# A four-layer decoder trunk on one core: the gate projection of the linear attention as seven products of halves

## The chip, the cores and the metric

The kernel runs on one core of one Trainium2 chip. The metric is the device time of one execution in microseconds (us). The engines are TensorE (PE; PEld is its weight load), VectorE (DVE), ScalarE (ACT), GpSimd (POOL) and SyncE (SP, which here only issues transfers).

## The reference, cut to what matters

Two decoder layers are computed for 256 positions of width 1024: first a gated linear attention (GLA) with a SwiGLU feed-forward network (FFN), then a block attention with its own FFN. The change touches only the gate `g` of the first layer:

```python
def gla_mixer(x, w_in, w_gk, b_gk, norm_g, w_out):
    q, k, v, g, gk_low = split_cols(x @ w_in, GLA_COLS)      # 512, 512, 1024, 1024, 16 columns
    ...
    o = from_heads(rms_norm(o.astype(x.dtype), norm_g)) * jax.nn.silu(g)
    return o @ w_out
```

So `g = x @ W` with x of 256 x 1024 and W of 1024 x 1024, all in float32.

## The kernel before

**Arithmetic.** A float32 product is made from three TensorE products of rounded numbers: each operand is split into a high part (a rounding copy on ACT) and a low part (a subtraction on DVE), and `mm3` sums high x high, low x high and high x low. One weight unit is 128 partitions x 1024 numbers (512 KB): one transfer by SP, one ACT copy (L265), one DVE subtraction (L266). The 256 positions are two row tiles t = 0, 1; columns come in blocks of 512.

**Order.** The kernel is written as a list of operations with reads and writes (`Plan.op`), and a planner (`Plan.emit`) orders each engine's queue ahead of time with costs written in the code: an operation takes the earliest start that its inputs, its engine and its buffers allow; ties go to what was written first; operations marked urgent may go ahead. Engines then run their queues in that fixed order. Buffers are 41 slots of 128 x 1024 numbers (`S`), eight PSUM banks (`acc` and `ps`, four each), and a buffer takes a slot only if enough are left for all unplaced buffers written before it. An accumulating transfer (`dma_add`) is issued by POOL; the planner gives it 1.3 us and lets its reader start 8 us later.

**The stage around the change**, in the order in which it is written: the values `v` block 0, the decay and keys and queries (up to L826), rotary tables, the second value block for row tile 0 (`v_block(1, 0)`), and then the loop at L881 over the row tiles: for t = 1 first `v_block(1, 1)`; the attention output `fo` into two `ps` banks (L891); its mean square (ACT L900, DVE L903, POOL L906); the two gate blocks `g_block` (24 matmuls each, then Silu on ACT, L878); the gated output `og` (DVE L916), its transposes (PE L925) and their split (ACT L929, DVE L933). The output projection `out_proj` with its eight weight rows `wo0` to `wo7` (split at L268, L269), a layer norm, and the FFN follow.

**The FFN already has the scheme that the change brings to the gates** (`seven`, L542): a product of a 2 x 2 block matrix by seven instead of eight block products (Winograd's form), with sums of x made by `x_sums` (DVE L458, L462, ACT L461) and sums of weights made in place, by DVE (`add_to`, L577) or by an accumulating transfer (`add_dma`, L583).

Of the kernel before, what the change touches and what calls it, by code (L numbers as in the profile page):

```python
# [12 lines left out]
ALU = mybir.AluOpType  # L13
# [3 lines left out]
P = 128  # L17
# [174 lines left out]
def kernel(ctx, tc, x, positions, gla_w_in, gla_w_gk, gla_b_gk, gla_norm_g, gla_w_out,  # L192
# [104 lines left out]
    def load_cols(name, w, c0):  # L297
        return [w_kcols(f"{name}{i}", w, 2 * i, 2, c0, 512) for i in range(KT // 2)]
# [11 lines left out]
    def transpose_split(src, dst, t, half, skey=None, dstf=None, dkey=None, n=4, keep=None):  # L310
        ps = pl.buf("ps", "tr")

        def tr():
            for j in range(n):
                k = 4 * half + j
                nc.tensor.transpose(ps.f[:, j * P:(j + 1) * P], src.f[:, k * P:(k + 1) * P], ident.f)  # L316
        pe(n * 256, tr, [(src, skey) if skey is not None else src, ident], [ps], urgent=True)

        def view(i):
            if dstf is not None:  # L320
                return dstf(i)
            return dst.ap[i][:, t, 4 * half:4 * half + 4, :]

        def hi():
            nc.scalar.copy(view(0), ps.f[:, 0:n * P].rearrange("p (k c) -> p k c", k=n))  # L325

        def lo():
            h, l = view(0), view(1)
            nc.vector.tensor_tensor(out=l, in0=ps.f[:, 0:n * P].rearrange("p (k c) -> p k c", k=n), in1=h.bitcast(F32),  # L329
                                    op=ALU.subtract)  # L330
        kh = dkey if dkey is not None else (t, half)
        if dstf is None:
            act(n * P, hi, [ps], [(dst, ("h",) + kh)], urgent=True)
            dve(n * P, lo, [ps, (dst, ("h",) + kh)], [(dst, ("l",) + kh)], urgent=True)
            if keep is not None:
                act(512, lambda: nc.scalar.copy(keep[t].f[:, 512 * half:512 * half + 512], ps.f), [ps],
                    [(keep[t], half)], urgent=True)
        else:
            dh, dl = dst
            act(n * P, hi, [ps], [(dh, kh)], urgent=True)  # L340
            dve(n * P, lo, [ps, (dh, kh)], [(dl, kh)], urgent=True)

    def Tk(T, t, k):
        return [(T, ("h", t, k // 4)), (T, ("l", t, k // 4))]
# [78 lines left out]
    def v_block(blk, t, T, ws, vt):  # L423
        ps = pl.buf("acc", f"v{blk}{t}")
        act_block(ps, T, ws, t)
        sl = slice(512 * blk, 512 * blk + 512)
        act(512, lambda: nc.scalar.copy(vt[t].f[:, sl], ps.f), [ps], [(vt[t], blk)])
# [249 lines left out]
    pl.op("SP", 0.8, lambda: None)  # L677
    load_x(0, 1, 2.9)
    for hf in range(2):
        transpose_split(xs[0], T0, 0, hf, skey=hf)  # L680
        if hf == 0:
            pl.op("PE", 0.6, busy(WARM[1]), [zeros, (xs[0], 0)], [junkps], urgent=True)
    for hf in range(2):
        load_x(1, hf, 2.9)
        transpose_split(xs[1], T0, 1, hf, skey=hf)
    wv0.append(split2("wv01", w0, 2, V0))
    wv0 += [w_kcols(f"wv0{i}", w0, 2 * i, 2, V0, 512) for i in range(2, KT // 2)]
    vps = [pl.buf("acc", f"v0{t}") for t in range(2)]
    for i in range(KT // 2):
        for t in range(2):  # L690
# [180 lines left out]
    og = [S_("og0"), S_("og1")]  # L871
    ogT = new_xT("ogT")

    def g_block(blk, t, ws):
        ps = pl.buf("acc", f"g{blk}{t}")
        act_block(ps, T0, ws, t)
        sl = slice(512 * blk, 512 * blk + 512)
        act(512, lambda: nc.scalar.activation(sg[t].f[:, sl], ps.f, AF.Silu), [ps], [(sg[t], blk)], table="silu")  # L878

    wgs = [load_cols("wg0", w0, G0), load_cols("wg1", w0, G0 + 512)]  # L880
    for t in range(2):  # L881
        if t == 1:
            v_block(1, 1, T0, wv1, v_sb)
        ob = [pl.buf("ps", f"o{t}{blk}") for blk in range(2)]
        for blk in range(2):
            def fo(blk=blk, t=t, ob=ob):
                for j in range(2):
                    h = 2 * blk + j
                    ops = [(scv(t), v_sb[t])] + ([(scv(2), v_sb[0])] if t else [])
                    for i, (s_, vt) in enumerate(ops):  # L890
                        nc.tensor.matmul(ob[blk].f[:, j * S:(j + 1) * S], s_[:, h, :], vt.f[:, h * S:(h + 1) * S],  # L891
                                         start=i == 0 and j == 0, stop=i == len(ops) - 1 and j == 1)
            pe(2048 * (1 + t), fo, [(scs[0], t), (v_sb[t], blk)] + ([(scs[1], 0), (v_sb[0], blk)] if t else []),
               [ob[blk]])
        ss, junk = pl.buf("m", "ss"), S_("junk")
        for blk in range(2):
            def fsq(blk=blk, ob=ob, ss=ss, junk=junk):
                for j in range(2):
                    h = 2 * blk + j
                    nc.scalar.activation(junk.f[:, h * S:(h + 1) * S], ob[blk].f[:, j * S:(j + 1) * S], AF.Square,  # L900
                                         accum_out=ss.f[:, h:h + 1])
            act(850, fsq, [ob[blk]], [(ss, blk), (junk, blk)])
        dve(10, lambda ss=ss: nc.vector.tensor_scalar(out=ss.f[:, 4:8], in0=ss.f[:, 0:4], scalar1=1.0 / GLA_DV,  # L903
                                                      scalar2=1e-6, op0=ALU.mult, op1=ALU.add),
            [(ss, 0), (ss, 1)], [(ss, 2)])
        pl.op("POOL", 0.6, lambda ss=ss: nc.gpsimd.tensor_tensor(  # L906
            out=ss.f[:, 8:12], in0=ss.f[:, 4:8], in1=mhalf.f.broadcast_to([P, 4]), op=ALU.pow),
            [(ss, 2), mhalf], [(ss, 3)])
        for blk in range(2):
            g_block(blk, t, wgs[blk])  # L910
        for blk in range(2):
            for j in range(2):
                def fog(blk=blk, j=j, t=t, ob=ob, ss=ss):
                    h = 2 * blk + j
                    hs = slice(h * S, (h + 1) * S)
                    nc.vector.scalar_tensor_tensor(out=og[t].f[:, hs], in0=ob[blk].f[:, j * S:(j + 1) * S],  # L916
                                                   scalar=ss.f[:, 8 + h:9 + h], in1=sg[t].f[:, hs],
                                                   op0=ALU.mult, op1=ALU.mult)
                dve(256, fog, [ob[blk], (ss, 3), (sg[t], blk)], [(og[t], (blk, j))], urgent=True)
            ps = pl.buf("ps", "trg")  # L920

            def trg(ps=ps, src=og[t], blk=blk):
                for j in range(4):
                    k = 4 * blk + j
                    nc.tensor.transpose(ps.f[:, j * P:(j + 1) * P], src.f[:, k * P:(k + 1) * P], ident.f)  # L925
            pe(4 * 256, trg, [(og[t], (blk, 0)), (og[t], (blk, 1)), ident], [ps], urgent=True)

            def gh(ps=ps, t=t, blk=blk):
                nc.scalar.copy(ogT.ap[0][:, t, 4 * blk:4 * blk + 4, :], ps.f.rearrange("p (k c) -> p k c", k=4))  # L929

            def gl(ps=ps, t=t, blk=blk):
                ks = slice(4 * blk, 4 * blk + 4)
                nc.vector.tensor_tensor(out=ogT.ap[1][:, t, ks, :], in0=ps.f.rearrange("p (k c) -> p k c", k=4),  # L933
                                        in1=ogT.ap[0][:, t, ks, :].bitcast(F32), op=ALU.subtract)
            act(512, gh, [ps], [(ogT, ("h", t, blk))], urgent=True)
            dve(512, gl, [ps, (ogT, ("h", t, blk))], [(ogT, ("l", t, blk))], urgent=True)

    gb = load_ln(0, 0)
    T1 = new_xT("xT1")
# [163 lines left out]
```

## Time and profile before

| | |
|---|---|
| median of 3 runs | 581.41 us (581.38 to 582.15) |
| the profiled execution | 580.57 us, of which the span from first to last instruction is 578.8 us |
| PE busy | 568.6 us, 98% of the span |
| DVE busy | 518.8 us, 90% |
| ACT busy | 352.5 us, 61% |
| granted TensorE clock | 0.998 of full speed |

PE and DVE are the two engines to watch. Busy shares are means over the span; the gate stage, which the change rewrites, is about 33 us of it.

### The profile page before, as it was taken

The page shows a single profiled execution, that of the slowest core. Times are in us where ns is not written, and L with a number is a line of the kernel's source. Part 1 is how long each engine was busy: PE and PEld are TensorE (multiplying, and loading weights), DVE is VectorE, ACT ScalarE, POOL GpSimd, SP SyncE. Part 2 cuts the span into 40 slices and gives each one's busy share as a digit, 9 for nine tenths or more (in the row PEclk, how much of TensorE's full clock was granted, in tenths as well). Part 3 has the DMA queues.
Part 4 walks back from the last instruction along what each step waited for, and adds up shares of the span by engine and source line. Part 5 has one row for each costly group of instructions (what it writes and reads, how often), then busy time and mean ns, then how long its engine had stood idle before and what let it go on. Part 6 is the DMA issues. An engine that isn't in the chain of part 4 may idle for free.

```text
span 578.8 us, 8048 instructions
## 1 busy us (share of the span) xinstructions
PE 568.6 (98%) x2980; PEld 485.6 (84%) x2980; DVE 518.8 (90%) x644; ACT 352.5 (61%) x469; POOL 45.3 (8%) x41
## 2 busy tenths in 40 slices
PE   9999999999999999999999999999999999999994
PEld 8898888888878888889889999888888788888883
DVE  5799467798999999999998789988989999999986
ACT  5696555346758586867454365734495767575720
POOL 1016000010010101000000000000101000010001
PEclk9999999999999999999999999999999999999999
DMA  9994286347896978869667445626867887877601
GB/s 289 352 327 145 76 265 244 110 129 234 265 217 224 257 236 239 209 215 285 215 212 228 160 144 179 208 74 218 215 203 221 213 286 176 307 179 236 183 1 72
DMA packets 57465, 119.38 MB, mean 206 GB/s; under 512 B 5265, under 2 KB 10801, under 8 KB 57426
## 3 DMA queue, kind: packets, MB, share of 16 engines
q1 hardware_dynamic: 51586, 108.84, 56.6%
q0 software_dynamic: 5408, 9.44, 10.1%
q10 hardware_dynamic: 432, 0.59, 0.3%
q8 instruction: 23, 0.38, 0.3%
q14 instruction: 16, 0.13, 0.1%
HBM read 117.81 MB, written 1.05 MB: 205 GB/s over the span
## 4 chain that ended last, share of the span: by engine, by line
PE 76%; DVE 9%; DMA 7%; ACT 3%; issue 3%; POOL 1%; DVEq 0%; ACTq 0%; SPq 0%
PE fy L303 6%; PE fy L301 6%; PE fy L302 6%; PE pa L560 4%; PE pa L559 4%; PE pa L557 4%; PE y L303 3%; PE y L302 3%; PE y L301 3%; DMA d0r<-in_ffn_w_down 2%; PE tr L316 2%; PE pc L557 2%; PE pc L560 2%; PE pc L559 2%; DVE A L577 2%
## 5 line engine op out<-in xcount | busy, mean ns | idle before, releaser
L577 DVE TENSOR_TENSOR A<-A,X 128x1024 f32<-128x1024 f32 x54 | 64.4, 1217 | 0.0
L583 POOL DMA_DIRECT2D X<-in_ffn_w_gu x18 | 22.2, 1261 | 261.2 <-PE fy L302 90.5
L325 ACT CAST xT<-tr 128x512 fp32r<-128x512 f32 x16 | 9.1, 590 | 31.1 <-PE tr L316 31.0
L372 POOL TENSOR_TENSOR st<-st,mhalf 128x1 f32<-128x1 f32 x8 | 7.6, 956 | 200.1 <-DVE st L370 200.1
L509 ACT CAST C0h<-X 128x1024 fp32r<-128x1024 f32 x10 | 10.5, 1051 | 16.8 <-DMA X<-in_ffn_w_gu 12.3
L509 ACT CAST B0h<-A 128x1024 fp32r<-128x1024 f32 x10 | 10.5, 1053 | 10.7 <-DVE A L577 10.7
L509 ACT CAST G0h<-A 128x1024 fp32r<-128x1024 f32 x10 | 10.5, 1052 | 6.8 <-DVE A L577 6.8
L509 ACT CAST A0h<-A 128x1024 fp32r<-128x1024 f32 x10 | 10.5, 1052 | 5.7 <-DMA A<-in_ffn_w_gu 5.5
L620 ACT ACTIVATE e<-pa 128x512 f32<-128x512 f32 (+1 forms) x10 | 5.5, 555 | 11.5 <-PE pa L560 11.5
L316 PEld LDWEIGHTS tr<-ident,e 128*128 128x128 f32 x72 | 8.7, 140 | 4.4 <-DVE e L621 1.9
L316 PE MATMUL tr<-ident,e 128*128 128x128 f32 x72 | 11.3, 274 | 1.0 <-DVE e L621 1.0
L509 ACT CAST D0h<-A 128x1024 fp32r<-128x1024 f32 x10 | 10.5, 1052 | 2.8 <-DVE A L577 2.8
L510 DVE TENSOR_TENSOR D0l<-A,D0h 128x1024 fp32r<-128x1024 f32 x10 | 12.2, 1219 | 0.0
L510 DVE TENSOR_TENSOR G0l<-A,G0h 128x1024 fp32r<-128x1024 f32 x10 | 12.2, 1218 | 0.0
L510 DVE TENSOR_TENSOR A0l<-A,A0h 128x1024 fp32r<-128x1024 f32 x10 | 12.2, 1218 | 0.0
L510 DVE TENSOR_TENSOR E0l<-X,E0h 128x1024 fp32r<-128x1024 f32 x10 | 12.2, 1218 | 0.0
L510 DVE TENSOR_TENSOR F0l<-X,F0h 128x1024 fp32r<-128x1024 f32 x10 | 12.2, 1218 | 0.0
L510 DVE TENSOR_TENSOR C0l<-X,C0h 128x1024 fp32r<-128x1024 f32 x10 | 12.2, 1217 | 0.0
L510 DVE TENSOR_TENSOR B0l<-A,B0h 128x1024 fp32r<-128x1024 f32 x10 | 12.2, 1216 | 0.0
L329 DVE TENSOR_TENSOR xT<-tr,xT 128x512 fp32r<-128x512 f32 x16 | 10.7, 684 | 1.5 <-ACT xT L325 0.9
L916 DVE SCALAR_TENSOR_TENSOR og<-o,ss,sg 128x256 f32<-128x256 f32 x8 | 3.6, 478 | 9.2 <-ACT sg L878 9.2
L364 DVE BATCH_NORM_STATS2 st<-r 128x6 f32<-128x512 f32 x16 | 11.1, 693 | 0.5
(1012 smaller groups left out, 2249.7 us busy)
## 6 DMA issues: line engine op xcount, KB each, us to landing
X<-in_ffn_w_gu SPq DMA_DIRECT2D x54, 512.0 KB, 4.8
A<-in_ffn_w_gu SPq DMA_DIRECT2D x18, 512.0 KB, 4.3
X<-in_ffn_w_gu POOLq DMA_DIRECT2D x18, 512.0 KB, 7.6
lng<-in_ln_g SPq DMA_DIRECT2D x4, 512.0 KB, 3.8
lnb<-in_ln_b SPq DMA_DIRECT2D x4, 512.0 KB, 5.4
x<-in_x SPq DMA_DIRECT2D x4, 256.0 KB, 3.8
fg00r<-in_ffn_w_gu SPq DMA_DIRECT2D x2, 512.0 KB, 6.6
fg01r<-in_ffn_w_gu SPq DMA_DIRECT2D x2, 512.0 KB, 7.0
```

Of the source, the lines that this page charges most:

```text
L301: nc.tensor.matmul(ps, lh, rh, start=start, stop=False)
L302: nc.tensor.matmul(ps, ll, rh, start=False, stop=False)
L303: nc.tensor.matmul(ps, lh, rl, start=False, stop=stop)
L316: nc.tensor.transpose(ps.f[:, j * P:(j + 1) * P], src.f[:, k * P:(k + 1) * P], ident.f)
L364: nc.vector.bn_stats(st.f[:, 6 * hf:6 * hf + 6], r.f[:, sl])
L509: act(1024, lambda: nc.scalar.copy(hi.r, raw.f), [raw], [hi])
L510: dve(1024, lambda: nc.vector.tensor_tensor(out=lo.r, in0=raw.f, in1=hi.f, op=ALU.subtract), [raw, hi], [lo])
L557: nc.tensor.matmul(ps.f[:, lo_], sh, wh.r[:, cs], start=first and q == 0 and j == 0, stop=False, skip_group_check=True)
L559: nc.tensor.matmul(ps.f[:, lo_], sl_, wh.r[:, cs], start=False, stop=False, skip_group_check=True)
L560: nc.tensor.matmul(ps.f[:, lo_], sh, wl.r[:, cs], start=False, stop=last_ and (q, j) == (units - 1, nk - 1), skip_group_check=True)
L577: dve(1024, lambda q=q, other=other: nc.vector.tensor_tensor(out=raws[q].f, in0=raws[q].f, in1=other.f, op=ALU.add), [raws[q], other], [ra ...
L583: nc.gpsimd.dma_start(uv(raws[q], n), unit(kh, gu, q, c0, n), accum_op=ALU.add)
```

## The change

The gate product is cut into halves: x into row tiles (t) and halves of its 1024 columns, W into halves of its rows (kh) and column blocks (cb). Instead of `g_block` for each t and cb (four blocks of 24 matmuls), `gate_seven` makes seven products of 12 matmuls, named after their left side (`a00`, `a01`, `s1`, `s2`, `s4`, `s3`, `a11`; `s` are sums of x). Three PSUM banks (pa, pb, pc) hold them. The sums of x are made by the FFN's `x_sums` from float32 copies of the transposed x, which ACT takes at the start (`xi32`). W's four quarters are used as seven right sides: three plain, four sums. Three of the four sums are accumulating transfers from memory (two units each, by POOL), one is a pair of DVE additions. Each right side is split anew into high and low parts. The second value block for t = 1, the gated output for t = 0 and the attention output for t = 1 come after the fifth product (`between`), and the first `fo` stays ahead of the gates.

```diff
+    xi32, x_t = [S_("x32i"), S_("x32j")], {}
...
-        transpose_split(xs[0], T0, 0, hf, skey=hf)
+        x_t[0, hf] = transpose_split(xs[0], T0, 0, hf, skey=hf)
...
+    for (t, hf), ps in x_t.items():
+        act(512, lambda t=t, hf=hf, ps=ps: nc.scalar.copy(xi32[t].f[:, 512 * hf:512 * hf + 512], ps.f),
+            [ps, wv0[3][0]], [(xi32[t], hf)])
...
-    def g_block(blk, t, ws):
-        ps = pl.buf("acc", f"g{blk}{t}")
-        act_block(ps, T0, ws, t)
-        sl = slice(512 * blk, 512 * blk + 512)
-        act(512, lambda: nc.scalar.activation(sg[t].f[:, sl], ps.f, AF.Silu), [ps], [(sg[t], blk)], table="silu")
-
-    wgs = [load_cols("wg0", w0, G0), load_cols("wg1", w0, G0 + 512)]
-    for t in range(2):
-        if t == 1:
-            v_block(1, 1, T0, wv1, v_sb)
+    def gate_seven(xsum, between):
+        pa, pc, pb = pl.buf("acc", "ga"), pl.buf("acc", "gc"), pl.buf("acc", "gb")
+        e1, e2 = sg
...
+        def load(kh, cb):
+            raws = [S_(f"gr{kh}{cb}{q}") for q in range(2)]
+            for q in range(2):
+                dma(lambda q=q: nc.sync.dma_start(uv(raws[q]), unit(kh, cb, q)), 512, [], [raws[q]])
+            return raws
+
+        def parts(raws):
+            out_ = []
+            for raw in raws:
+                hi, lo = S_("gwh", True), S_("gwl", True)
+                act(1024, lambda raw=raw, hi=hi: nc.scalar.copy(hi.r, raw.f), [raw], [hi])
+                dve(1024, lambda raw=raw, hi=hi, lo=lo: nc.vector.tensor_tensor(
+                    out=lo.r, in0=raw.f, in1=hi.f, op=ALU.subtract), [raw, hi], [lo])
+                out_.append((hi, lo))
+            return out_
+
+        def add(raws, others):
+            for r_, o_ in zip(raws, others):
+                dve(1024, lambda r_=r_, o_=o_: nc.vector.tensor_tensor(out=r_.f, in0=r_.f, in1=o_.f, op=ALU.add),
+                    [r_, o_], [r_])
+
+        def add_dma(raws, kh, cb):
+            for q in range(2):
+                dma_add(lambda q=q: nc.gpsimd.dma_start(uv(raws[q]), unit(kh, cb, q), accum_op=ALU.add), [raws[q]],
+                        [raws[q]])
+
+        def product(ps, left, ws, first, last_):
+            st, rd = lhs(left)
+            for q, (wh, wl) in enumerate(ws):
...
+                pe(6 * 512, f, rd + [wh, wl], [ps])
...
+        w00 = load(0, 0)
+        product(pa, "a00", parts(w00), True, False)
+        keep_(pa, e1, 0)
+        add_dma(w00, 0, 1)
+        w10 = load(1, 0)
+        product(pb, "a01", parts(w10), True, True)
+        combine(e1, 0, pb, ALU.add)
+        silu(e1, 0)
+        w11 = load(1, 1)
+        product(pc, "s1", parts(w00), True, False)
+        keep_(pc, e2, 0)
+        add(w00, w11)
+        w11s = parts(w11)
+        add_dma(w11, 0, 1)
+        product(pa, "s2", parts(w00), False, False)
+        keep_(pa, e1, 1)
+        add_dma(w00, 1, 0)
+        product(pc, "s4", w11s, False, True)
+        combine(e1, 1, pc, ALU.subtract)
+        silu(e1, 1)
+        between()
+        product(pa, "s3", parts(w11), False, False)
+        combine(e2, 0, pa, ALU.subtract, flip=True)
+        silu(e2, 0)
+        product(pa, "a11", parts(w00), False, True)
+        silu(e2, 1, pa)
...
+    heads = {0: head_out(0)}
+    xsum = x_sums(xi32)
+
+    def between():
+        v_block(1, 1, T0, wv1, v_sb)
+        gated(0, *heads[0])
+        heads[1] = head_out(1)
+    gate_seven(xsum, between)
+    gated(1, *heads[1])
```

`head_out` and `gated` hold the code of the old loop's first and second half. `keep_` is an ACT copy of a PSUM bank (128 x 512), `combine` a DVE operation with one PSUM and one SBUF input (128 x 512), `silu` an ACT activation; all three are urgent.

## Rows read from the trace of the kernel before

**Rows 1.** The page: busy time, share and instructions of each engine.
```profile
PE 568.6 (98%) x2980; PEld 485.6 (84%) x2980; DVE 518.8 (90%) x644; ACT 352.5 (61%) x469; POOL 45.3 (8%) x41
```
**Rows 2.** The longest waits of PE after its start: total, times, longest.
```profile
PE tr L316 <- DVE e L621: 1.0, 2, 0.6
PE scx L824 <- POOL kx L797: 0.4, 1, 0.4
```
**Rows 3.** Busy time of each engine in stretches between stages.
```profile
20.00:43.00 23.00, 23.00 (x184) 22.36 (x184) 20.38 (x33) 19.57 (x22) 2.19 (x5) 1.00 0.98 328
43.00:57.50 14.50, 14.06 (x96) 12.89 (x95) 14.50 (x18) 9.74 (x12) 9.09 (x2) 1.00 0.42 145
57.50:90.30 32.80, 32.80 (x150) 27.28 (x150) 17.15 (x21) 18.10 (x34) 2.04 (x2) 1.00 0.60 197
90.30:119.00 28.70, 28.70 (x133) 23.43 (x132) 22.95 (x34) 12.07 (x16) 1.98 (x2) 1.00 0.50 166
119.00:150.00 31.00, 31.00 (x146) 25.74 (x145) 29.01 (x34) 20.24 (x28) 2.58 (x2) 1.00 0.64 185
150.00:260.00 110.00, 109.41 (x496) 90.09 (x495) 109.81 (x109) 77.29 (x89) 8.58 (x7) 1.00 0.80 231
```
**Rows 4.** Timeline of PE in the gate stage (start, duration, line, operation).
```profile
64.13 0.39 PE L301 MATMUL g<-wg10h,xT 128*128 128x512 f32 x1
...
69.57 0.60 PE L925 MATMUL trg<-ident,og 128*128 128x128 f32 x4
...
75.98 0.59 PE L891 MATMUL o<-v,sc 128*128 128x256 f32 x2
...
79.24 0.58 PE L301 MATMUL g<-wg00h,xT 128*128 128x512 f32 x1
...
90.33 0.60 PE L925 MATMUL trg<-ident,og 128*128 128x128 f32 x4
```
**Rows 5.** Timeline of DVE: successive operations of each size, and the first FFN split.
```profile
58.49 1.21 DVE L266 TENSOR_TENSOR wg13l<-wg13r,wg13h 128x1024 fp32r<-128x1024 f32 x1
59.62 1.27 DVE L269 SCALAR_TENSOR_TENSOR wo0l<-wo0r,normg,wo0h 128x1024 fp32r<-128x1024 f32 x1
...
126.43 0.68 DVE L462 TENSOR_TENSOR s3hl<-s,s3hl 128x512 fp32r<-128x512 f32 x1
127.03 0.68 DVE L534 TENSOR_TENSOR sil<-pu,sil 128x512 f32<-128x512 f32 x1
```
**Rows 6.** Timeline of ACT: the decay weights, successive splits, a PSUM copy.
```profile
13.32 1.06 ACT L707 CAST wgkhl<-wgkr 128x1024 fp32r<-128x1024 f32 x1 [0.17 <-DMA wgkr<-in_gla_w_in]
...
47.86 1.04 ACT L265 CAST wg10h<-wg10r 128x1024 fp32r<-128x1024 f32 x1
48.80 1.04 ACT L265 CAST wg11h<-wg11r 128x1024 fp32r<-128x1024 f32 x1
...
108.41 0.59 ACT L336 COPY x32a<-tr 128x512 f32<-128x512 f32 x1
```
**Rows 7.** Timeline of PE: first reader of the decay weights.
```profile
19.23 2.08 PE L718 MATMUL gk<-xT,wgkhl 128*128 128x256 f32 x16
```
**Rows 8.** Line 583, the FFN's accumulating transfers: POOL's issue, and from issue to landing.
```profile
L583 POOL DMA_DIRECT2D X<-in_ffn_w_gu x18: 1203/1207/1392, 126.0 to 538.9; - x18
...
DMA to landing us min/median/max: 5.9/7.6/10.9
```
**Rows 9.** Timeline of POOL before the gate stage.
```profile
42.56 5.60 POOL L794 COPY kx<-ke 128x256 f32<-128x256 f32 x1
49.15 3.94 POOL L797 COPY kx<-qd 128x256 f32<-128x256 f32 x1 [0.99 <-DVE qd L775]
```
**Rows 10.** Timeline of SP's issues: the last weight row of the output projection.
```profile
74.85 0.38 SPq L262 DMA_DIRECT2D wo7r<-in_gla_w_out  x1
```
**Rows 11.** Timeline of DVE in the FFN: the split D1.
```profile
142.37 1.22 DVE L510 TENSOR_TENSOR D1l<-A,D1h 128x1024 fp32r<-128x1024 f32 x1
```
**Rows 12.** Timeline of PE in the FFN: its use of D1's low part.
```profile
148.09 0.39 PE L560 MATMUL pa<-D1l,s2hl 128*128 128x512 f32 x1
```

More of the change, by code (lines that the diff above doesn't have):

```diff
@@ L341, in transpose_split @@
             dve(n * P, lo, [ps, (dh, kh)], [(dl, kh)], urgent=True)
+        return ps
     def Tk(T, t, k):
@@ L684 @@
         load_x(1, hf, 2.9)
-        transpose_split(xs[1], T0, 1, hf, skey=hf)
+        x_t[1, hf] = transpose_split(xs[1], T0, 1, hf, skey=hf)
     wv0.append(split2("wv01", w0, 2, V0))
     wv0 += [w_kcols(f"wv0{i}", w0, 2 * i, 2, V0, 512) for i in range(2, KT // 2)]
+    for (t, hf), ps in x_t.items():
+        act(512, lambda t=t, hf=hf, ps=ps: nc.scalar.copy(xi32[t].f[:, 512 * hf:512 * hf + 512], ps.f),
+            [ps, wv0[3][0]], [(xi32[t], hf)])
     vps = [pl.buf("acc", f"v0{t}") for t in range(2)]
@@ L872, with lhs, unit, uv @@
     ogT = new_xT("ogT")
-    def g_block(blk, t, ws):
-        ps = pl.buf("acc", f"g{blk}{t}")
-        act_block(ps, T0, ws, t)
-        sl = slice(512 * blk, 512 * blk + 512)
-        act(512, lambda: nc.scalar.activation(sg[t].f[:, sl], ps.f, AF.Silu), [ps], [(sg[t], blk)], table="silu")
-    wgs = [load_cols("wg0", w0, G0), load_cols("wg1", w0, G0 + 512)]
-    for t in range(2):
-        if t == 1:
-            v_block(1, 1, T0, wv1, v_sb)
+    def gate_seven(xsum, between):
+        pa, pc, pb = pl.buf("acc", "ga"), pl.buf("acc", "gc"), pl.buf("acc", "gb")
+        e1, e2 = sg
+        def lhs(n):
+            if n[0] == "s":
+                return (lambda k: (xsum[n].r[:, k * P:(k + 1) * P], xsum[n].r[:, 512 + k * P:512 + (k + 1) * P]),
+                        [(xsum[n], 0), (xsum[n], 1)])
+            t, kh = int(n[1]), int(n[2])
+            return (lambda k: (T0.ap[0][:, t, 4 * kh + k, :], T0.ap[1][:, t, 4 * kh + k, :]),
+                    [(T0, ("h", t, kh)), (T0, ("l", t, kh))])
+        def unit(kh, cb, q):
+            k0 = 4 * kh + 2 * q
+            return w0[k0 * P:(k0 + 2) * P, G0 + 512 * cb:G0 + 512 * cb + 512].rearrange("(k p) c -> p k c", p=P)
+        def uv(b):
+            return b.f.rearrange("p (k c) -> p k c", k=2)
+        def load(kh, cb):
[23 more added lines that the diff above has]
+            for q, (wh, wl) in enumerate(ws):
+                def f(q=q, wh=wh, wl=wl):
+                    for j in range(2):
+                        sh, sl_ = st(2 * q + j)
+                        cs = slice(512 * j, 512 * j + 512)
+                        nc.tensor.matmul(ps.f, sh, wh.r[:, cs], start=first and q == 0 and j == 0, stop=False,
+                                         skip_group_check=True)
+                        nc.tensor.matmul(ps.f, sl_, wh.r[:, cs], start=False, stop=False, skip_group_check=True)
+                        nc.tensor.matmul(ps.f, sh, wl.r[:, cs], start=False, stop=last_ and q == 1 and j == 1,
+                                         skip_group_check=True)
+                pe(6 * 512, f, rd + [wh, wl], [ps])
+        def keep_(ps, dst, j):
+            sl = slice(512 * j, 512 * j + 512)
+            act(512, lambda: nc.scalar.copy(dst.f[:, sl], ps.f), [ps], [(dst, j)], urgent=True)
+        def combine(dst, j, ps, op, flip=False):
+            sl = slice(512 * j, 512 * j + 512)
+            def f():
+                a0, a1 = (dst.f[:, sl], ps.f) if flip else (ps.f, dst.f[:, sl])
+                nc.vector.tensor_tensor(out=dst.f[:, sl], in0=a0, in1=a1, op=op)
+            dve(512, f, [ps, (dst, j)], [(dst, j)], urgent=True)
+        def silu(dst, j, ps=None):
+            sl = slice(512 * j, 512 * j + 512)
+            act(512, lambda: nc.scalar.activation(dst.f[:, sl], ps.f if ps else dst.f[:, sl], AF.Silu),
+                [ps] if ps else [(dst, j)], [(dst, j)], table="silu", urgent=True)
+        w00 = load(0, 0)
[24 more added lines that the diff above has]
+        silu(e2, 1, pa)
@@ L884, with head_out, fo @@
+    def head_out(t):
         ob = [pl.buf("ps", f"o{t}{blk}") for blk in range(2)]
         for blk in range(2):
-            def fo(blk=blk, t=t, ob=ob):
+            def fo(blk=blk):
                 for j in range(2):
@@ L896, with fsq @@
         for blk in range(2):
-            def fsq(blk=blk, ob=ob, ss=ss, junk=junk):
+            def fsq(blk=blk):
                 for j in range(2):
@@ L902 @@
             act(850, fsq, [ob[blk]], [(ss, blk), (junk, blk)])
-        dve(10, lambda ss=ss: nc.vector.tensor_scalar(out=ss.f[:, 4:8], in0=ss.f[:, 0:4], scalar1=1.0 / GLA_DV,
-                                                      scalar2=1e-6, op0=ALU.mult, op1=ALU.add),
+        dve(10, lambda: nc.vector.tensor_scalar(out=ss.f[:, 4:8], in0=ss.f[:, 0:4], scalar1=1.0 / GLA_DV,
+                                                scalar2=1e-6, op0=ALU.mult, op1=ALU.add),
             [(ss, 0), (ss, 1)], [(ss, 2)])
-        pl.op("POOL", 0.6, lambda ss=ss: nc.gpsimd.tensor_tensor(
+        pl.op("POOL", 0.6, lambda: nc.gpsimd.tensor_tensor(
@@ L907, with gated, fog @@
             out=ss.f[:, 8:12], in0=ss.f[:, 4:8], in1=mhalf.f.broadcast_to([P, 4]), op=ALU.pow),
             [(ss, 2), mhalf], [(ss, 3)])
+        return ob, ss
+    def gated(t, ob, ss):
         for blk in range(2):
-            g_block(blk, t, wgs[blk])
-        for blk in range(2):
+            part = blk ^ t
             for j in range(2):
-                def fog(blk=blk, j=j, t=t, ob=ob, ss=ss):
+                def fog(blk=blk, j=j, part=part):
                     h = 2 * blk + j
                     hs = slice(h * S, (h + 1) * S)
+                    gs = slice(512 * part + j * S, 512 * part + (j + 1) * S)
@@ L916, in fog @@
                     nc.vector.scalar_tensor_tensor(out=og[t].f[:, hs], in0=ob[blk].f[:, j * S:(j + 1) * S],
-                                                   scalar=ss.f[:, 8 + h:9 + h], in1=sg[t].f[:, hs],
+                                                   scalar=ss.f[:, 8 + h:9 + h], in1=sg[t].f[:, gs],
                                                    op0=ALU.mult, op1=ALU.mult)
-                dve(256, fog, [ob[blk], (ss, 3), (sg[t], blk)], [(og[t], (blk, j))], urgent=True)
+                dve(256, fog, [ob[blk], (ss, 3), (sg[t], part)], [(og[t], (blk, j))], urgent=True)
@@ L920, with trg, gh @@
             ps = pl.buf("ps", "trg")
-            def trg(ps=ps, src=og[t], blk=blk):
+            def trg(ps=ps, blk=blk):
                 for j in range(4):
                     k = 4 * blk + j
-                    nc.tensor.transpose(ps.f[:, j * P:(j + 1) * P], src.f[:, k * P:(k + 1) * P], ident.f)
+                    nc.tensor.transpose(ps.f[:, j * P:(j + 1) * P], og[t].f[:, k * P:(k + 1) * P], ident.f)
             pe(4 * 256, trg, [(og[t], (blk, 0)), (og[t], (blk, 1)), ident], [ps], urgent=True)
-            def gh(ps=ps, t=t, blk=blk):
+            def gh(ps=ps, blk=blk):
@@ L929, in gh, with gl @@
                 nc.scalar.copy(ogT.ap[0][:, t, 4 * blk:4 * blk + 4, :], ps.f.rearrange("p (k c) -> p k c", k=4))
-            def gl(ps=ps, t=t, blk=blk):
+            def gl(ps=ps, blk=blk):
                 ks = slice(4 * blk, 4 * blk + 4)
```

## The prediction, as recorded before the run

> **What bounds the kernel now.** I read the page's busy times first. PE is busy 568.6 of 578.8 us [rows 1]: whatever shortens the kernel must take work from PE or one of its few pauses. The waits of PE come next: apart from its start it stood still 1.0 us for two DVE results in the FFN and 0.4 us for a POOL copy just ahead of the gate stage [rows 2]. Then the busy times by stage. In the gate stage (57.5 to 90.3 us) PE is busy all 32.80 us, DVE only 17.15 and ACT 18.10; up to 119 us, through the output projection and the layer norms, PE is still full and DVE has 22.95 of 28.7. Two neighbours look different: from 43 to 57.5 DVE is full (14.50 of 14.50), and in the FFN from 150 to 260 both are, PE 109.41 and DVE 109.81 of 110 [rows 3]. So matmuls taken out of the gates count in full, if DVE, which pays for them, gets its extra work done in the idle time between 57.5 and 119 us and enters the FFN no later than PE does.
>
> **What is removed.** The gates now take 2 row tiles x 2 column blocks x 8 row blocks x 3 = 96 matmuls of 128x512; seven products of 4 x 3 make 84. Twenty-four of them took 64.13 to 69.57 us [rows 4], 0.2267 us each: 12 x 0.2267 = 2.72 us less on PE. Transposes, `fo` and the value block only change place.
>
> **What is added on DVE.** Splits go from 8 to 14 units, +6; the weight addition is 2 operations of the same size. Successive ones start 1.13 us apart [rows 5]: 8 x 1.13 = 9.0 us. `x_sums` has 8 operations of half the size and `combine` 3; those start 0.60 us apart [rows 5]: 11 x 0.60 = 6.6. Together 15.7 us. (A `combine` has one operand in PSUM, as the row at 127.03 has.) The idle time between 57.5 and 119 us is 15.65 + 5.75 = 21.4 us [rows 3]; the stretch shrinks by 2.72, so about 3.0 us of slack stay. It fits, barely. The cover is this idle time alone: what doesn't find its place there arrives late in the FFN. There DVE idled another 1.99 us before 150 [rows 3], and its split D1, ended at 143.6, is read at 148.09 [rows 11, 12], a lead of 4.5 us that can be eaten before PE stops.
>
> **What is added on ACT.** Six splits at 0.94 us and eleven half-size copies (4 `xi32`, 4 in `x_sums`, 3 `keep_`) at 0.59 [rows 6]: 5.6 + 6.5 = 12.1 us. ACT idles 4.76 us from 43 to 57.5 and 14.7 us in the gate stage [rows 3]; hidden. The `xi32` copies come early: 4 x 0.59 = 2.4 us ahead of the decay weights' copy, which then starts at 15.7 instead of 13.32 and ends at 16.8 [rows 6]; PE first reads these at 19.23 [rows 7]. It costs nothing within that margin of 2.4 us.
>
> **Where x_sums goes.** Its inputs are there from about 16 us on, so the planner lets it run wherever DVE is free. From 20 to 43 us DVE idles 2.6 us [rows 3], half of what it needs (4.8); the rest falls into the full stretch 43 to 57.5. What is queued behind it there: keys, the copies kx on POOL (5.60 and 3.94 us, the second ending at 53.1 [rows 9]) and PE's `scx`, which already waits 0.4 us [rows 2]. On the other side DVE has six splits to make before 59.6 instead of eight, 2.3 us less. Bounds: from the 0.4 us gained to 2.2 us (4.8 - 2.6) lost; I take 0, since the planner can place the second half of `v_block(1, 0)` in front.
>
> **Accumulating transfers.** Three sums in two units each are 6 issues on POOL of 1.21 us, 7.3 us; POOL is busy 2.04 us in the stage [rows 3, 8]. Each lands 5.9 to 10.9 us after its issue, median 7.6 [rows 8]. They make a chain, and PE needs something else to do meanwhile. In times of the kernel before: POOL is free of kx at 53.1 [rows 9]; w00's two accumulations land at 60.7 and 61.9; two splits, some 3.2 us with ACT's part: s1 ready at about 65. Addition of w11, 2.3 us: 67.3. Splits: s2 ready at about 69.6. Then w00's second accumulation, to 78.4, and a11 ready at about 81. For w11 the accumulation starts at 67.3 and lands at 76.1: s3 ready at about 78. PE: a00 and a01 (24 matmuls, 5.4 us) and a half of `fo` end at about 63.6; `v_block(1, 1)` has all inputs and fills 5.4 us to 69.0; s1, s2, s4 at 2.72 each end at 77.2. So s1 has 4 us of slack, s2 some 2 us, s3 comes about 1 us late, and a11, which the transposes (0.9) and the second `fo` (3.26 us, 75.98 to 79.24 in [rows 4]) can precede, has some 3 us. The second `fo` is no filler any earlier: the four `ps` banks are two for the first `fo`, held until its gates are through, and two reserved for the transposes. Stall in the stage: from 0 to 1 us by these rows, and by the longest landing (10.9) more, which is a rival. I take 0.4, what the wait for kx costs today.
>
> **The end of the stage.** The last gates are off the path: row tile 0 of the output projection needs only `gated(0)`. The weight rows `wo` get their slots later than now (the last is issued at 74.85 [rows 10]), because unplaced gate parts reserve slots ahead of them; wv1's eight slots come free at about 69 in compensation, and DVE needs 1.13 to 1.21 us a row where PE uses 1.4 (six matmuls). I take 0 and count what goes wrong there under the first rival. Memory traffic rises by four units (12 instead of 8); the queues have room here (197 GB/s against 328 from 20 to 43 us [rows 3]).
>
> **Sum.** -2.72 + 0.4 = -2.3 us. The profiled execution took 580.57, so it would take 578.3; the median of the runs is 0.84 above it, so the median goes to 579.1. About 0.2% (1.2 us) is what can be told from no change.
>
> **The rivals.**
>
> *DVE becomes the bound.* DVE's idle time between dependent steps doesn't vanish because there is work elsewhere: while it waits for accumulations it can only take what has a slot, and the `wo` rows have none yet. If half of the gate stage's 15.65 us stays idle, 7.8 instead of 3.0, DVE enters the FFN 4.8 us late; 2.0 are absorbed there, 2.8 fall on the lead of 4.5 us. PE stalls 0 to 2.8 us: 579.1 to 581.9. Against it: the lead is larger than the rest.
>
> *The accumulations starve (slower).* POOL may be slow while DVE runs without pause: its plain copies of 128x256 took 5.60 and 3.94 us while DVE was full [rows 3, 9]. If each accumulation takes the longest 10.9 us instead of 7.6, the two in series on w11 bring s3 to about 84.6 against PE's 77.2; `v_block(1, 1)` is used up and the queue is fixed, so PE waits up to 7.4 us less what the planner's own 9.3 us had put ahead of s3 (some 3.4 us): 4 us. 581.41 - 2.72 + 4 + 0.4 = 583.1; it decides from 1.5 us a transfer on. Against it: issues of 1.20 to 1.39 us and a median of 7.6 us in an FFN whose DVE is 99.8% busy [rows 3, 8]. The Trainium skill has a rule for this (SBUF — State Buffer, section SBUF: two separate sides): a transfer issued by GpSimd may sit idle because its descriptors can't be written while VectorE holds the port pair that they share. By that rule the time would be that of this rival, or more; the landing times of [rows 8] speak against it for the operations that DVE runs here.
>
> *More than the matmuls.* The fixed order changes, and the waits of 1.0 and 0.4 us [rows 2] go away, with no new one: 581.41 - 2.72 - 1.4 = 577.3.
>
> *Nothing arrives.* The change shifts the planner's order in the FFN, where PE and DVE are both full; a pause of 2 to 3 us there, like the two of 1.0 us in all today, takes the gain: about 581.
>
> **How the numbers follow.** Forecast 0.58 (578.2 to 580.2, point 579.1); DVE bound 0.12; starving 0.14; more 0.07; nothing arrives 0.09. The range 577.7 to 583.0 takes in DVE bound, nothing arrives and half of starving. Faster by over 0.2% (under 580.2): 0.58 + 0.07 less a little at the edge = 0.63. Same: most of DVE bound and of nothing arrives, and the edge, 0.19. Slower (over 582.6): starving and the tail of DVE bound, 0.18.
>
> **What would show it.** 84 instead of 96 gate matmuls at 0.227 us and the stage's end (the transposes now at 90.33 [rows 4]) near 88.0. DVE near 31 of 32 us busy between 57 and 88, or else idle there with PE waiting behind L510-like splits of gate parts. Issue to landing of the six accumulations: near 7.6 for the forecast, above 9.1 for starving. The first FFN transposes 2.3 us earlier, and D1's lead above 2 us. Wrong it would be by a PE wait of over 1.5 us in front of s1, s2 or s3, or by one in the FFN that isn't there today.

## The result and the profile after

Five runs of each kernel: 589.44 us after (586.92 to 589.50) against 581.73 before (581.38 to 583.07), ratio 1.0113, 95% interval [1.0093, 1.0133]. The change makes the kernel 1.1% slower (7.7 us), outside the predicted range of 577.7 to 583.0. The profiled execution is the shortest of the five, 586.92 us, 6.35 above that of before; the last 1.4 us of the medians' distance is in no trace.

The page of the changed kernel, busy times and DMA queues:

```profile
PE 570.2 (97%) x2968; PEld 483.1 (83%) x2968; DVE 533.6 (91%) x663; ACT 363.2 (62%) x486; POOL 54.1 (9%) x47
...
q1 hardware_dynamic: 51042, 107.79, 55.5%
q0 software_dynamic: 7040, 12.58, 12.8%
```

PE has its 12 instructions less and yet 1.6 us more busy time than in [rows 1], in part from matmuls that ran at a lower clock (below). DVE has its 14.8 us more (15.7 predicted), ACT 10.7 (12.1). The queue lines (packets, MB, share of the 16 engines) come back below. The stretches of [rows 3], changed kernel (busy us of PE, PEld, DVE, ACT, POOL; granted clock; DMA share; GB/s; the share adds up the times of all packets, and packets that overlap can take it a little above 1):

```profile
20.00:43.00 23.00, 23.00 (x185) 22.36 (x184) 20.97 (x35) 19.72 (x22) 2.23 (x5) 1.00 0.75 248
43.00:57.50 14.50, 14.50 (x98) 13.31 (x98) 14.50 (x21) 9.66 (x14) 9.60 (x3) 1.00 0.24 74
57.50:90.30 32.80, 30.47 (x136) 24.30 (x134) 23.95 (x27) 21.07 (x38) 10.42 (x8) 1.00 1.02 283
90.30:119.00 28.70, 26.85 (x112) 20.59 (x113) 25.42 (x34) 16.99 (x22) 0.98 (x1) 0.94 0.61 193
119.00:150.00 31.00, 31.00 (x147) 25.69 (x146) 27.67 (x35) 16.09 (x24) 3.43 (x3) 1.00 0.70 200
150.00:260.00 110.00, 108.55 (x491) 89.29 (x490) 109.40 (x109) 75.40 (x88) 7.32 (x6) 1.00 0.79 233
```

In the gate stage PE is no longer full, and DVE is not what stops it: it is busy 23.95 of 32.8. What has filled up is the last but one column, the transfer engines, from 0.60 to 1.02. Not all of that is accumulation: up to 57.5 us the engines now move less than in [rows 3] (248 and 74 GB/s against 328 and 145), and loads that were done by then now come later. The waits of PE and of ACT in the changed kernel, 57 us on (total, times, longest):

```profile
PE y L301 <- ACT ogT L1033: 2.1, 1, 2.1
PE ga L933 <- DVE sg L949: 0.6, 1, 0.6
PE ga L936 <- DVE gwl L911: 0.5, 1, 0.5
PE trg L1029 <- DVE og L1020: 0.4, 1, 0.4
PE y L302 <- DVE ogT L1037: 0.4, 2, 0.2
```
```profile
ACT gwh L910 <- DMA gr<-in_gla_w_in: 11.3, 4, 4.1
```

PE's list doesn't name the cause: it waits for `ogT`, ACT's copy of the transposed gated output, which the output projection multiplies. One engine back it is there: ACT stood 11.3 us in four waits for `gr`, the blocks into which the transfers accumulate. POOL's issues of these (L923; 6.2, 11.1 and 16.3 us to landing at least, at median and at most, against [rows 8]):

```profile
56.54 2.59 POOL L923 DMA_DIRECT2D gr<-in_gla_w_in  x2 [3.90 <-ACT s4hl L462]
...
69.31 1.25 POOL L923 DMA_DIRECT2D gr<-in_gla_w_in  x1 [6.13 <-issue]
74.41 2.44 POOL L923 DMA_DIRECT2D gr<-in_gla_w_in  x2 [3.85 <-ACT ogT L1033]
77.12 1.20 POOL L923 DMA_DIRECT2D gr<-in_gla_w_in  x1 [0.27 <-DVE gwl L911]
```

And how a late block reaches PE, ACT and then PE in the changed kernel:

```profile
89.08 1.04 ACT L910 CAST gwh<-gr 128x1024 fp32r<-128x1024 f32 x1 [3.23 <-DMA gr<-in_gla_w_in]
90.04 0.58 ACT L1033 CAST ogT<-trg 128x512 fp32r<-128x512 f32 x1
```
```profile
84.44 0.60 PE L1029 MATMUL trg<-ident,og 128*128 128x128 f32 x4
...
88.12 0.40 PE L936 MATMUL ga<-gwl,s3hl 128*128 128x512 f32 x1
90.67 0.49 PE L301 MATMUL y<-wo4h,ogT 128*128 128x512 f32 x1 [2.15 <-ACT ogT L1033]
91.39 0.80 PE L302 MATMUL y<-wo4h,ogT 128*128 128x512 f32 x1 [0.23 <-DVE ogT L1037]
...
94.12 0.63 PE L302 MATMUL y<-wo1h,ogT 128*128 128x512 f32 x1
94.55 0.52 PE L303 MATMUL y<-wo1l,ogT 128*128 128x512 f32 x1
94.91 0.39 PE L301 MATMUL y<-wo2h,ogT 128*128 128x512 f32 x1
```

The copy for the output projection had its input since 85 (the transposes `trg` from 84.44 on), but stands in ACT's fixed queue behind a split of the next sum, which is in flight. PE pauses 2.15 us, and then its matmuls follow each other at 0.43 us instead of 0.23 (91.99 to 94.12; the granted clock was 0.50 from 92.0 to 94.5, 1.2 GHz, the lower of TensorE's two levels): nine matmuls from 90.67 to 94.91 took 4.24 us, 2.1 at full clock.

The account at the first FFN product (`pg`), 114.46 us before and 119.08 after: 4.6 us late, where 2.3 early was forecast. PE's waits in the stage are 4.0 us, the slow clock 1.9 (the 4.24 us less 2.1 and less the wait of 0.2), the product s2 stretched from 2.72 to 3.88 us (74.03 to 77.91) 0.7 beyond the wait that the list counts; with -2.72 that makes 3.9, and 0.7 is spread. By the end of the span the delay is 6.3; of the 1.7 added there, 0.3 is in the waits of the transposes of `e` (1.3 us against 1.0 in [rows 2]), the rest in no single place.

### The profile page after: what moved, and what is told of

Its sections match the earlier page's. It is cut to its first block, busy times and chain, and to the rows that moved or that the text cites. A ratio compares the mean times of both kernels' runs of the same rounds, so it can differ in the third digit from the quotient of the medians.

```text
span 585.1 us, 8060 instructions
## 1 busy us (share of the span) xinstructions
PE 570.2 (97%) x2968; PEld 483.1 (83%) x2968; DVE 533.6 (91%) x663; ACT 363.2 (62%) x486; POOL 54.1 (9%) x47
## 3 DMA queue, kind: packets, MB, share of 16 engines
HBM read 119.90 MB, written 1.05 MB: 207 GB/s over the span
## 4 chain that ended last, share of the span: by engine, by line
PE 69%; DVE 3%; issue 0%; DVEq 0%
PE fy L303 6%; PE fy L302 6%; PE fy L301 6%; PE pa L561 5%; PE pa L560 5%; PE pa L558 5%; PE pc L558 3%; PE pc L561 3%; PE pc L560 3%; PE tr L316 2%; PE mq L303 1%; PE mq L302 1%; PE mk L303 1%; PE mk L302 1%; PE mk L301 1%; PE mq L301 1%
## 5 line engine op out<-in xcount | busy, mean ns | idle before, releaser
L910 ACT CAST gwh<-gr 128x1024 fp32r<-128x1024 f32 x14 | 14.4, 1048 | 11.3 <-DMA gr<-in_gla_w_in 11.3
L911 DVE TENSOR_TENSOR gwl<-gr,gwh 128x1024 fp32r<-128x1024 f32 x14 | 16.8, 1214 | 4.7 <-ACT gwh L910 4.7
L510 ACT CAST G0h<-A 128x1024 fp32r<-128x1024 f32 x10 | 10.5, 1053 | 13.4 <-DVE A L578 10.1
L510 ACT CAST C0h<-X 128x1024 fp32r<-128x1024 f32 x10 | 10.5, 1050 | 12.6 <-DMA X<-in_ffn_w_gu 12.6
L510 ACT CAST B0h<-A 128x1024 fp32r<-128x1024 f32 x10 | 10.5, 1052 | 11.0 <-DVE A L578 11.0
L510 ACT CAST A0h<-A 128x1024 fp32r<-128x1024 f32 x10 | 10.5, 1052 | 3.9 <-DMA A<-in_ffn_w_gu 3.8
L567 ACT COPY e<-pa 128x512 f32<-128x512 f32 (+1 forms) x20 | 10.8, 541 | 2.7 <-PE pa L561 2.7
L511 DVE TENSOR_TENSOR E0l<-X,E0h 128x1024 fp32r<-128x1024 f32 x10 | 12.1, 1215 | 0.0
L365 DVE BATCH_NORM_STATS2 st<-r 128x6 f32<-128x512 f32 x16 | 11.1, 693 | 0.5
L383 DVE SCALAR_TENSOR_TENSOR xn<-r,st,lnb 128x512 f32<-128x512 f32 x16 | 11.3, 745 | 0.0
## 6 DMA issues: line engine op xcount, KB each, us to landing
gr<-in_gla_w_in POOLq DMA_DIRECT2D x6, 512.0 KB, 11.1
```

The source lines that it names most:

```text
L510: act(1024, lambda: nc.scalar.copy(hi.r, raw.f), [raw], [hi])
L511: dve(1024, lambda: nc.vector.tensor_tensor(out=lo.r, in0=raw.f, in1=hi.f, op=ALU.subtract), [raw, hi], [lo])
L911: dve(1024, lambda raw=raw, hi=hi, lo=lo: nc.vector.tensor_tensor(out=lo.r, in0=raw.f, in1=hi.f, op=ALU.subtract), [raw, hi], [lo])
```

## The experiments

Theory: the accumulating transfers hold the transfer engines (traffic). Rivals: starved descriptors on POOL, the order or the planner's cost, VectorE, the chain of sums in itself.

**1. The neighbours' bytes away.** The rows `wo` and the units of the first FFN column block are loaded with 64 columns instead of 1024; splits and matmuls run on a constant block.

```diff
+            if tiny is not None:
+                nc.sync.dma_start(hraw.f[:, 0:64], tiny)
+                return
```

> The changed kernel with the same order on every engine, but the eight weight rows of the output projection and the eight units of the first FFN block move 32 KB each instead of 512 KB (their splits read a constant tile, so that part of the result is not the reference's). If the six accumulations are late because the DMA engines are full of these loads (traffic), they land in 6 to 8 us (median now 11.1, longest 16.3), ACT waits for them 2 us or less in all instead of 11.3, PE loses no more than 1 us between 57 and 119 us, and the time is 580 to 582. If DVE's steady work starves them (starving), the landing times stay near 11 to 16 us and the time near 587 to 589, since DVE does the same work.

Measured: 583.11 us, ratio 1.0027 [1.0014, 1.0041]. The six accumulations land in 6.1 to 11.8 us, median 7.7, as in [rows 8], and PE is full again in the gate stage (32.79 of 32.80 us). Of the 1.13% lost, 0.27% remain, though DVE and POOL do what they did: it is not their work that made the landings late. Traffic is not the whole either: the time is above the 582 expected of it, ACT still waits 6.1 us for `gr`, where 2 or less was expected, and from 90.3 to 119 us PE is busy 27.50 of 28.70.

**2. The same bytes without accumulation.** Same order and same queue; the six transfers are plain copies, so the sums are not formed.

```diff
-nc.gpsimd.dma_start(uv(raws[q]), unit(kh, cb, q), accum_op=ALU.add)
+nc.gpsimd.dma_start(uv(raws[q]), unit(kh, cb, q))
```

> The changed kernel with the six accumulating transfers made plain copies from the same queue, same bytes read, same order (the three sums are left out, so the gates are not the reference's). If the accumulation itself costs DMA time (traffic, with its doubled price), the queue of POOL takes about half the share and the six land in 6 to 9 us; time 582 to 585. If the way by POOL's queue is what is slow (starving), nothing changes: 11 us median, 587 to 589.

Measured: 580.71 us, ratio 0.9979 [0.9968, 0.9989]: 1.3% (8 us) from one operand of six instructions, and faster than the 582 to 585 us expected of traffic. The six land in 4.3 to 10.5 us, median 7.5, and take half the engine time: 14.1% of the 16 engines from 50 to 115 us, against 27.5% in the changed kernel. The stage in this run:

```profile
57.50:90.30 32.80, 32.80 (x150) 27.21 (x149) 28.73 (x33) 26.24 (x43) 7.58 (x7) 1.00 0.96 340
90.30:119.00 28.70, 28.70 (x138) 23.36 (x137) 28.10 (x40) 14.96 (x21) 1.99 (x2) 1.00 0.62 198
```

PE never stops, ACT waits 0.9 us for `gr`, and the engines move 340 GB/s where the changed kernel moved 283 at a higher share. `pg` starts at 111.44, 3.0 us before that of the kernel before. Not all of it arrives: the profiled execution has lost it by the span's end (579.0 against 578.8), and over all executions the ratio leaves 0.21%, 1.2 us.

**3. The planner is told 14 us instead of 8** for these six.

> The changed kernel with the planner told that a gate accumulation's reader can start 14 us after the issue instead of 8, nothing else. If the loss comes from queues whose fixed order waits for late data (ACT's copies of the sums ahead of other copies), the planner now puts other work in front and PE's pauses of 4.2 us and the low clock shrink: 581 to 584. If the late data itself is the limit (there is no other work to put in front), 586 to 589.

Measured: 591.29 us, ratio 1.0168 [1.0151, 1.0185]; `pg` at 123.27. That is above both expected ranges. The planner did put other work in front: ACT no longer waits for `gr` at all. But the last accumulation is now issued at 83.7 instead of 77.1, landing takes 12.6 us at the median, and PE, whose waits are spread over seven places, is busy only 22.70 of 28.70 us from 90.3 to 119. A higher cost in the planner did not mend the loss; other values were not tried.

**4. The order alone.** Eight products in the new order (`between` after the fourth, head outputs as in the change), no sums.

> The gates by eight products of halves in the new order (first attention output ahead, second value block and the gated output of row tile 0 between), no sums, no accumulations, 96 matmuls. If the order alone costs nothing, the time is that of the kernel before, 581 to 582.5; the whole loss then belongs to the sums. If the new order is at fault, 585 or more.

Measured: 582.40 us, ratio 1.0009 [0.9997, 1.0020]; `pg` at 114.70. The order costs nothing that can be told.

**5. All four weight sums by VectorE**, from four plainly loaded blocks.

```diff
-        add_dma(w00, 0, 1)
+        w01 = load(0, 1)
+        add(w00, w01)
...
-        add_dma(w11, 0, 1)
+        add(w01, w11)
...
-        add_dma(w00, 1, 0)
+        add(w00, w10)
```

> The seven products as in the changed kernel, but all four weight sums are made by VectorE from four plainly loaded blocks; no transfer accumulates. Traffic theory: the three accumulations put 6 units of 0.52 MB at twice the transfer time into 57 to 88 us; without them the DMA share of 57.5 to 90.3 falls from 1.02 to about 0.7, ScalarE's waits for the weight blocks from 11.3 us to under 2, TensorE loses under 1 us between 57 us and the first FFN product, which starts at 112 to 113 us, and the time is 579 to 582, ratio 0.995 to 1.001. VectorE theory: six more sums of 1.22 us make 7.3 us more, 31.3 of 32.8 us in 57.5 to 90.3; if that is the bound, TensorE waits 3 us or more for gwl and gr, the first FFN product is not before 115 and the time is 583 to 586.

Measured: 579.76 us, ratio 0.9971 [0.9959, 0.9984]; `pg` at 112.48.

```profile
57.50:90.30 32.80, 32.02 (x148) 26.35 (x147) 31.78 (x37) 29.06 (x47) 4.08 (x2) 1.00 0.75 259
90.30:119.00 28.70, 28.70 (x136) 23.34 (x135) 28.43 (x39) 12.06 (x16) 1.98 (x2) 1.00 0.56 176
```

VectorE is busy 31.78 of 32.80 us, and PE loses one wait of 0.8. The transfer share is 0.75, as expected; against 0.60 in the kernel before, with no accumulation in the stage, that is the part that later loads bring. VectorE had the room.

**6. One sum by transfer, off the chain.** As 5, but the sum for s3 accumulates into a loaded block that nothing has read (`add_dma(w01, 1, 1)` behind `add(w00, w01)`, as in the FFN), used by PE 22 us after its issue.

> As the run with all sums by VectorE, but the sum for s3 is an accumulating transfer into a loaded block that nothing has read yet, as the FFN does it, so that it can be issued before the products begin; three sums by VectorE. Traffic theory: two accumulations of 0.52 MB at twice the time, issued before 60 us, land in 6 to 9 us and are wanted only near 85: the same time as with all sums by VectorE within 0.5 us, the first FFN product at 112 to 113.5. Theory that any accumulation in this stage makes data late: it lands after 12 us or more and the first FFN product is later by over 2 us than without it.

Measured: 579.23 us, ratio 0.9958 [0.9941, 0.9975]; issue at 59.37, landing 8.3 us, `pg` at 111.75, PE 32.60 and 28.70 us busy in the two stretches. Same time as 5 within its interval, and 1.55% (9 us) faster than the changed kernel.

**7. The sums of x alone**, in the kernel before, used by nothing.

> The kernel before, with the four ScalarE copies of x's transposes and the sums and differences of x and their splits added and used by nothing: the price of these alone. If they are hidden (the prediction's 0): 578.5 to 579.5 us of span and a ratio of 0.999 to 1.001. If they delay q, k and the scores at 46 to 57 us, where VectorE and ScalarE are busy: the first gate product moves from 57.56 by 0.5 to 2 us and the ratio is 1.001 to 1.004.

Measured: 581.91 us, ratio 1.0003 [0.9992, 1.0015]. Hidden in the time, as predicted, but not without a trace: the first gate product comes at 59.68 instead of 57.56, because the planner puts six matmuls of `v_block(1, 1)` ahead of it, and `pg` is at 114.32, about where it was (114.46). (The profiled execution's span, 580.6, is above the 578.5 to 579.5 expected; it is one execution, and the ratio is from ten.)

**8. The sums of x behind the first weight splits.**

```diff
-    xsum = x_sums(xi32)
...
         add_dma(w00, 0, 1)
+        xsum.update(x_sums(xi32))
         w10 = load(1, 0)
```

> The changed kernel with the sums of x called behind the splits of the first weight block, not ahead of them. If the first pair of accumulations is late for that order (56.5 us instead of 53.1 predicted), it is issued 1 to 3 us earlier and s1, s2 and what follows come earlier: 584 to 587 us against 589.4, ratio 1.004 to 1.009. If the traffic of the later four accumulations beside the loads of wo and of the first FFN block is what counts: 588 to 590, ratio 1.010 to 1.014, with ScalarE's waits for the weight blocks near 11 us as before.

Measured: 586.18 us, ratio 1.0076 [1.0061, 1.0091]. The first pair is issued at 52.94 instead of 56.54 and 2 to 3 us come back (by the ratios 0.37%, by the medians 3.3), a little less than the pair gained; in the two profiled executions `pg` moves by only 0.8, from 119.08 to 118.25; ACT's waits for `gr` shrink to 2.9 us, but now waits for the rows of `wo` (3.0 and 1.5 us) stand in ACT's queue and PE waits 3.5 us for the copy of `v` behind them. The DMA share stays 1.02.

**9 and 10. Traffic without a chain.** Run 5, and beside it the six transfers of the changed kernel, at the same places, into spare blocks that nothing reads: once accumulating, once plain.

```diff
+        def beside(ws, kh, cb):
+            for q in range(2):
+                b = S_(f"sp{kh}{cb}{q}")
+                gps(500, lambda b=b: nc.gpsimd.memset(b.f, 0.0), list(ws[q]), [b])
+                pl.op("POOL", 1.3, lambda q=q, b=b: nc.gpsimd.dma_start(uv(b), unit(kh, cb, q), accum_op=ALU.add),
+                      list(ws[q]), [b], extra=8.0)
```

> The run with all four sums by VectorE, and beside it the six accumulating transfers of the changed kernel (the same bytes, the same POOL queue, each released by the same splits) into spare blocks that GpSimd has set to zero and that nothing reads: the traffic without the chain of data. If the traffic alone costs the time (the loads of wo and of the first FFN block come late because accumulated bytes hold the transfer engines): the DMA share of 57.5 to 90.3 goes from 0.75 to 1.0 or more, the first FFN product comes 2 to 5 us later than 112.48, 582 to 585, ratio 1.001 to 1.006. If it is the chain (each sum is wanted by the next split, and waits 6 to 16 us for its landing): within 0.6 us of the run without them, 579 to 580.5, ratio 0.996 to 0.9985.

> The same with six plain copies in place of the six accumulating transfers. If an accumulated byte takes twice the transfer time of a copied one, queue 0 takes about half the share that it takes with accumulation (by some 1.6% of 16 engines' span for 3.1 MB, not 2.7 to 3%), the DMA share of 57.5 to 90.3 stays below 1.0 or the rate is higher by 40 GB/s or more, and the time is within 0.6 us of the run without them; if the transfers cost the same, shares and times of the two runs are the same.

Measured: 588.95 us accumulating, ratio 1.0121 [1.0102, 1.0140], and 582.49 plain, ratio 1.0005 [0.9995, 1.0015]. The two have the same order on every engine, and no engine reads what these transfers bring: 6.5 us is the price of accumulating alone. `pg` comes at 121.17 against 114.46. Three expectations failed. The loss is larger than the 582 to 585 us expected of traffic. The DMA share from 57.5 to 90.3 is 0.88, not 1.0 or more, because it falls to 0.20 from 64 to 70 us between two busy stretches. And the plain run is itself 0.34% (2.0 us, by the ratios) over run 5: the spare blocks shift the order on PE, DVE and ACT, with 1.9 us of waits for the gate's buffer `sg` in both runs. The queues from 50 to 115 us, accumulating run first:

```profile
q1 hardware_dynamic: 3904, 10.49, 45.7%
q0 software_dynamic: 1632, 3.15, 27.4%
```
```profile
q1 hardware_dynamic: 4541, 11.72, 49.5%
q0 software_dynamic: 864, 3.15, 14.2%
```

The same 3.15 MB took 27.4% of the engines' 65 us accumulating and 14.2% copied, in 1632 packets against 864: twice the engine time per byte, 17.8 us against 9.2 of all 16 engines. The stretches of the two runs after 82 us, accumulating first:

```profile
82.00:88.00 6.00, 4.51 (x22) 3.48 (x21) 5.80 (x9) 5.37 (x13) 1.30 (x1) 1.00 1.08 300
88.00:94.00 6.00, 5.92 (x29) 4.33 (x27) 5.26 (x8) 3.51 (x5) 0.70 (x1) 1.00 1.07 318
94.00:100.00 6.00, 5.39 (x24) 3.77 (x22) 2.97 (x3) 2.30 (x3) 0.00 (x0) 1.00 1.04 397
100.00:106.00 6.00, 2.60 (x6) 2.12 (x7) 4.54 (x5) 5.19 (x6) 0.00 (x0) 0.69 0.65 223
```
```profile
82.00:88.00 6.00, 4.51 (x23) 3.47 (x22) 5.93 (x9) 5.36 (x13) 1.16 (x1) 1.00 1.03 405
88.00:94.00 6.00, 5.95 (x28) 4.39 (x27) 5.13 (x7) 5.03 (x7) 0.83 (x1) 1.00 1.03 391
94.00:100.00 6.00, 6.00 (x28) 4.57 (x27) 6.00 (x7) 5.06 (x6) 0.00 (x0) 1.00 0.71 263
100.00:106.00 6.00, 6.00 (x27) 4.82 (x27) 5.86 (x10) 1.05 (x1) 0.48 (x1) 1.00 0.57 175
```

Both are at a share above 1.0, full; with accumulation full means 300 GB/s, without 405. (From 94 to 100, when no accumulation is under way any more, the accumulating run moves 397.) The backlog is worked off 6 us later, and in that time PE meets an output projection whose row `wo6` is not split: ACT waits 3.2 us for the FFN's first unit `fg00`, which its queue has ahead of the copy `ogT`, VectorE waits for that copy with the split of `wo6` behind it, and PE 4.0 us for the split:

```profile
98.49 1.05 ACT L265 CAST fg00h<-fg00r 128x1024 fp32r<-128x1024 f32 x1 [3.18 <-DMA fg00r<-in_ffn_w_gu]
101.46 0.69 DVE L1051 TENSOR_TENSOR ogT<-trg,ogT 128x512 fp32r<-128x512 f32 x1 [4.49 <-ACT ogT L1047]
```
```profile
PE y L303 <- DVE wo6l L269: 4.0, 1, 4.0
```

Then its clock falls (a mean of 0.69 from 100 to 106).

## Why the prediction was wrong

**The step that failed is the one on the accumulating transfers' traffic: "the queues have room here", from 197 GB/s against 328 [rows 3].** It compared bytes; what fills up is the engines' time. The page of the kernel before had the price in two lines that I didn't divide (queues; packets, MB, share):

```profile
q1 hardware_dynamic: 51586, 108.84, 56.6%
q0 software_dynamic: 5408, 9.44, 10.1%
```

A loaded megabyte took 0.52% of the span, an accumulated one 1.07%. By these lines the six accumulations (3.15 MB) take 3.4% of 578.8 us, 19.5 us of all 16 engines, and one loaded quarter less gives back 1.05 x 0.52% = 3.2 us: 16 us more work in a stretch of 32.8 us that was 0.60 busy, that is 1.1 (1.02 was measured, with the later loads in it, and the rest ran on behind the stage). A full stage could have been worked out ahead. The change against run 2 and run 9 against run 10 have the same order on every engine each and differ in the accumulation alone: it is this and no property of the order.

**The landing time went with it.** 7.6 us is what an accumulation takes when the engines have room, in the FFN [rows 8] and here without its neighbours' bytes (7.7, run 1). In the full stage it was 11.1 at the median. My rival for slow landings had the right sign, the right symptom (above 9.1 us) and about the right place, but the wrong cause: the transfers didn't starve for VectorE. The Trainium skill's rule weighed there (SBUF — State Buffer, section SBUF: two separate sides) is not what happened: in run 1 VectorE was busier in the two stretches (54.4 us against 49.4) and they landed fast. I had also left out the rule's condition: the page ties it to VectorE operations in a two-port mode, and says that `tensor_tensor`, the operation of the gates' splits and sums, has none. What the Trainium skill says of an accumulate elsewhere (DMA: Bandwidth & Descriptors, section Rules for kernel authors), that it reads its destination and writes it later, fits a doubled engine time; which part of it costs, or whether the doubled number of packets does, no run here separates.

**The stall went another way than thought.** I looked for PE waits in front of s1, s2 and s3. Those were short (0.5 us at s2). The data's delay passed through ACT's fixed queue to work that didn't need the data: a copy for the output projection.

**The first pair was late for a reason of its own.** I had POOL free at 53.1 and the accumulations issued then. They were issued at 56.54, because the sums of x, which I had costed at nothing, ran ahead of the first splits on DVE. As DVE time they are free (run 7), but their place delayed the head of a chain by 3.6 us, and run 8 got 2 to 3 us of the time back.

**What held.** Twelve matmuls less; the work added to DVE and ACT within 1.5 us; the `xi32` copies and the order free; DVE has the room, even for three more sums (run 5). With the weight sums taken from the transfers (runs 5 and 6) the kernel is 0.29% and 0.42% faster, 1.7 and 2.4 us, where -2.3 was forecast. By the ratios most of the gain at `pg` arrives there (2.0 us at `pg` in run 5, 2.7 in run 6). In run 2 it does not: 3.0 us at `pg`, 1.2 at the end. So the rival "nothing arrives" is true for a part in that run; there the waits of the transposes `tr` for VectorE's `e` are 2.5 us against 1.0 [rows 2]. In runs 5 and 6 these waits are 0.5 and 1.2, and nothing shows that rival.

**What stays open.** How the loss of the changed kernel divides between the traffic and the chain: the traffic alone costs 6.5 us (9 against 10), accumulating instead of copying in the chain 8 (the change against 2), and without the neighbours' bytes the chain still leaves it 4 us behind run 6 (0.69% between the ratios of 1 and 6); these overlap. How much of the full stage is later loads and how much accumulation is told only by run 5's 0.75 beside 1.02. Whether run 6's single accumulation is free because it is one or because it is early was not tried.

## What to carry to other kernels

Cost a transfer in the engines' time, share divided by megabytes for each queue of the page, before asking whether there is room: here an accumulated byte counted twice. An addition that a busy compute engine still had room for was cheaper here than an accumulation in a stage whose transfers are near full, and the one accumulation that cost nothing here was issued early, into a block that nothing else needed until then. Where queues are ordered ahead of time, a late block delays what stands behind its reader; look one engine behind the wait that the list of PE names.

## What the runs showed of the hardware

With the transfer engines full, accumulation brought the rate down from 405 to 300 GB/s (runs 10 and 9, 82 to 88 us), and an accumulated unit of 512 KB came as 272 packets where a copied one came as 144 (1632 and 864 for six). POOL's issue of one accumulation took 1.20 to 1.54 us (changed kernel), of the plain copy 0.72 to 0.90 (run 2). The output projection's pauses of 2.2 us (changed kernel, from 88.5) and 4.0 us (run 9, from 99.4) were each followed by matmuls 0.43 us apart instead of 0.23, at the lower of TensorE's two levels, 1.2 GHz; the granted clock was 0.50 from 92.0 to 94.5 in the changed kernel and from 103.4 to 108.5 in run 9.
